# A two-layer encoder trunk: each layer's first projection is v by token tile in place of q and k by halves

## The chip, the cores and the metric

The kernel runs on one core of one Trainium2 chip. A core has a matrix engine (TensorE, PE in the profile), a vector engine (VectorE, DVE), an activation engine (ScalarE, ACT), a general engine (GpSimd, POOL) and a synchronisation engine (SyncE, SP), which here issues nearly all DMAs. Every engine works off its own list of instructions in order; semaphores hold one engine back for another. The metric is the device time of one execution in microseconds (us), the median of several; lower is better.

## The reference, cut to what matters

There is one sequence of 512 tokens with 1024 features, float32, and two layers.

```python
for l in range(DEPTH):                       # 2
    h = rms_norm(x, norm_mix_pre[l], NORM_EPS)
    m = hybrid_mixer(h, w_in[l], w_a[l], w_b[l], w_out[l], lam[l], subln_g[l], cos, sin, lambda_init)
    x = x + rms_norm(m, norm_mix_post[l], NORM_EPS)
    h = rms_norm(x, norm_ffn_pre[l], NORM_EPS)
    f = swiglu(h, w_gate_up[l], w_down[l])
    x = x + rms_norm(f, norm_ffn_post[l], NORM_EPS)
```

`hybrid_mixer` projects h by `w_in` into q, k and v of a differential attention (4 heads with two maps each, `softmax(q0 k0) - lam_full * softmax(q1 k1)`, then a norm with gain `subln_g`), into q, k and v of three groups of windowed attention, and into gates. All q and k are rotated by position (cos, sin). The two attention results go through `w_a` and `w_b`, are gated, added, and projected by `w_out`.

## The kernel before, in words

**Matmuls.** Every product of two fp32 matrices is made of three matmuls on a high and a low part of each operand (high by high, low by high, high by low). A weight block of 256 columns of `w_in` is one DMA of 1 MB into one of two `raw` buffers (`load_raw`, line 88); `split_part` (lines 92 to 112) makes its high part on ACT (`whi`, L106 or L109) and its low part on DVE (`wlo`, L107 or L110). `Stream` (lines 133 to 167) holds the order of the blocks: `cut` splits one and issues the load of the next, `get` hands one out.

**Pre-norm.** A tile is 128 tokens. `prenorm_scale` (lines 242 to 246) squares and sums a tile on ACT (L244), takes the root on DVE and POOL (L73, L75) and scales the tile on DVE (L246). `prenorm_turn` (lines 248 to 256) transposes it on PE in 8 blocks (L252), casts the high part on ACT (L254) and subtracts for the low part on DVE (L255). The result `hTh`, `hTl` has the tokens as columns and is the operand of all projections of a layer. In the head of the program these steps stand in a block in which the ACT and DVE orders are written by hand (lines 395 to 408).

**Projections.** `ws_gen` (lines 199 to 207) multiplies two weight halves with all 512 tokens: 48 matmuls of 512 columns, with a yield after every 12. `ws_halves` (lines 212 to 224) does two such projections with 256 tokens at a time, q and k of the first half, then of the second, so that only the tiles 0 and 1 are needed at first; `between` puts the transposes of tiles 2 and 3 behind the first two pieces. `proj_v` (lines 468 to 480) makes v of a tile with 24 matmuls of 256 columns, and yields after each tile. q and k then go through `rope` (lines 435 to 449): four products on DVE (L446) and two sums on POOL (L447, L448). `split_of` casts the rotated pair on ACT (L485) and subtracts on DVE (L486) for the scores of three of the groups.

**Attention between projections.** `drive` calls `att_step` at every yield of a projection. Each attention is a generator (`da_attn`, `g_attn`) that puts in one step per yield. For a tile of 128 queries, `scores` stands at step 0, `turn` (transposes, L537) at 3, `values` (L546) at 5 and `finish` (transposes of the normed output, L564) at 7; the next tile follows 4 steps later. The scores' 24 matmuls (L511) are followed by the maxima on DVE (L517), exponentials on ACT (L519) and the difference of two maps on DVE (L525, L527). `DELAY` says how many yields lie between an attention's last operand and its first step; its fifth number is added for the first differential attention of a layer.

**Order.** PE's instructions stand as they are written. Those of DVE and ACT are ordered by a scheduler when the program is built, outside of blocks written by hand; `SPLIT_PRI` lets weight splits go ahead.

**Between layers and at the end.** `act_stationary` (lines 293 to 326) is the product with `w_down`, whose last part goes tile by tile; `post` then adds the normed result to x (L267 to L280) and does the next pre-norm. It ends with `ws_halves` of the next two blocks, here q and k of the next layer. The last layer's tiles go out in four DMAs of 32 rows each, by SP (L283).

Of the kernel before, what the change touches and what calls it, by code (L numbers as in the profile page):

```python
# [17 lines left out]
P = 128  # L18
D = 1024
S = 512  # L20
SPLIT_PRI = 400
DELAY = (1, 3, 1, 1, 2)
KT = D // P
NT = S // P
HID = 2816
# [8 lines left out]
def encoder_trunk_kernel(  # L34
# [197 lines left out]
    def class_rows(t, n):  # L232
        return t.rearrange("(t s r) c -> r s t c", s=4, r=4)[n]
# [24 lines left out]
    def postnorm_tile(n, pe, src, g, dst, src_perm, dst_perm, xt=None):  # L258
        if xt is None:
            xt = m4([P, D])  # L260
            rows_in(xt, src, n, src_perm)
        t = m4([P, D])
        ss2 = small(2)
        first, ms = small(1), small(1)

        def msum(ss2):
            nc.vector.scalar_tensor_tensor(out=ms, in0=ss2[:, 1:2], scalar=1.0 / D, in1=first,  # L267
                                           op0=ALU.mult, op1=ALU.add)
            return ms

        for e in range(2):
            sl = slice(e * S, (e + 1) * S)
            nc.scalar.activation(out=junk, in_=pe[e], func=AF.Square, accum_out=ss2[:, e:e + 1])
            if e == 0:
                nc.vector.tensor_scalar(out=first, in0=ss2[:, 0:1], scalar1=1.0 / D, scalar2=NORM_EPS,
                                        op0=ALU.mult, op1=ALU.add)
            nc.vector.tensor_tensor(out=t[:, sl], in0=pe[e], in1=g[:, sl], op=ALU.mult)
        r = small(1)
        nc.gpsimd.tensor_tensor(out=r, in0=msum(ss2), in1=mhalf[:, 0:1], op=ALU.pow)  # L279
        nc.vector.scalar_tensor_tensor(out=xt, in0=t, scalar=r, in1=xt, op0=ALU.mult, op1=ALU.add)  # L280
        if dst_perm:
            for s in range(4):
                nc.sync.dma_start(out=class_rows(dst, n)[s], in_=xt[32 * s:32 * s + 32, :])  # L283
        else:
            nc.sync.dma_start(out=dst[n * P:(n + 1) * P, :], in_=xt)
        return xt, t
# [3 lines left out]
        hTl = pp.tile([P, KT, S], F32R, tag="hTl", name=nm("hTl"))  # L290
        return hTh, hTl

    def act_stationary(nk, lhs, post, turn, next_jobs):
        accs = [[pj(), pj()], [pj(), at(0)], [at(1), at(2)], [at(3), at(4)]]
        nch = nk // 2
        held = []

        def step(n, e, k, hi, lo):
            ah, al = lhs(k, n)
            sl = slice(e * S, (e + 1) * S)  # L300
            o = accs[n][e]
            nc.tensor.matmul(o, ah, hi[:, sl], start=(k == 0), stop=False)  # L302
            nc.tensor.matmul(o, al, hi[:, sl], start=False, stop=False)  # L303
            nc.tensor.matmul(o, ah, lo[:, sl], start=False, stop=(k == nk - 1))  # L304

        for c in range(nch):
            ks = [(2 * c + kk,) + w for kk, w in enumerate(stream.get())]
            if c >= nch - 2:
                held += ks
                continue  # L310
            for kk in ks:
                for n in range(NT):
                    for e in range(2):
                        step(n, e, *kk)
        with (tc.manual_schedule(engines={mybir.EngineType.Activation, mybir.EngineType.DVE})
              if turn is None else nullcontext()):
            for n in range(NT):
                for e in range(2):
                    for kk in held:
                        step(n, e, *kk)  # L320
                    if turn is not None and e == 0 and n >= 2:
                        turn(n - 2)
                post(n, accs[n])
        if turn is None:
            return None
        return ws_halves(next_jobs, 2, {(0, 0): lambda: turn(2), (0, 1): lambda: turn(3)})

    def hT_pairs(hT):
        return [(hT[0][:, k, :], hT[1][:, k, :]) for k in range(KT)]
# [9 lines left out]
    def specs():  # L339
# [10 lines left out]

        for l in range(depth):
            for u in range(2):
                yield from qkv(l, 256 * u, 512 + 256 * u, 1024 + 256 * u)[(1 if l == 0 and u == 0 else 0):]
            for u in range(2):
                for gi in range(3):
                    b = GB + gi * 1536 + 256 * u
                    q, k, v = qkv(l, b, b + 512, b + 1024)
                    yield from (k, v, q) if gi == 0 else (q, k, v)

            def gates(c):  # L360
                return [win(l, ZC + 256 * c, "cols"), win(l, ZC + D + 256 * c, "cols")]
# [24 lines left out]
    nc.sync.dma_start(out=ts0[2][0:1, :], in_=norm_mix_pre[0].unsqueeze(0))  # L386
    rows_in(xt0[0], x0, 0, True)
    nc.sync.dma_start(out=ident, in_=ident_d)
    rows_in(xt0[1], x0, 1, True)
    first_raw = load_raw([wcols(0, w_in, 0)])  # L390
    rows_in(xt0[2], x0, 2, True)
    rows_in(xt0[3], x0, 3, True)
    ones = ts0[1][0:1, 0:P]
    first_w = []
    with tc.manual_schedule(engines={mybir.EngineType.Activation, mybir.EngineType.DVE}):
        nc.vector.memset(ones, 1.0)
        for e in range(2):
            gb = at(e)
            nc.tensor.matmul(gb, ones, ts0[2][0:1, e * S:(e + 1) * S], start=True, stop=True)
            nc.scalar.copy(out=g[:, e * S:(e + 1) * S], in_=gb)  # L400
        prenorm_scale(xt0[0], ts0[0], g)
        prenorm_scale(xt0[1], ts0[1], g)
        prenorm_turn(0, ts0[0], *hT)
        first_w.append(split_part(first_raw, "rope", 0, 0.125))
        prenorm_turn(1, ts0[1], *hT)
        first_w.append(split_part(first_raw, "rope", 1, 0.125))
        prenorm_scale(xt0[2], ts0[2], g)
        prenorm_scale(xt0[3], ts0[3], g)
    head.close()
    hrhs = hT_pairs(hT)  # L410
    first = ws_halves([lambda: (lhs_cols(first_w), hrhs), lambda: (lhs_cols(stream.get()), hrhs)], 2,
                      {(0, 0): lambda: prenorm_turn(2, ts0[2], *hT), (0, 1): lambda: prenorm_turn(3, ts0[3], *hT)})

    for l in range(depth):
        lam_init = 0.8 - 0.6 * math.exp(-0.3 * l)
# [6 lines left out]

        cosb = ip.tile([P, S], F32, tag="cos", name=nm("cos"))
        sinb = ip.tile([P, S], F32, tag="sin", name=nm("sin"))

        def rt():
            return ip.tile([P, 2, S], F32, tag="r", name=nm("r"), bufs=3)
# [29 lines left out]

        oaT = [big() for i in range(2)]

        def proj_qk(which, first):  # L460
            if first is None:
                return (yield from ws_gen(lhs_cols(stream.get()), hrhs))
            if which == 0:
                nc.sync.dma_start(out=cosb, in_=cos_t)
                nc.sync.dma_start(out=sinb, in_=sin_t)
            return first[which]

        def proj_v():
            w2 = stream.get()
# [9 lines left out]
                nc.scalar.copy(out=v[:, 2 * n2:2 * n2 + 2, :], in_=o)  # L479
            return v  # L480

        def split_of(which, natural, first=None):
            pair = rope((yield from proj_qk(which, first)), natural, rt())
            hi, lo = op(), op()
            nc.scalar.copy(out=hi, in_=pair)  # L485
            nc.vector.tensor_tensor(out=lo, in0=pair, in1=hi.bitcast(F32), op=ALU.subtract)  # L486
# [11 lines left out]
            return [(q[0], k[0]), (q[0], k[1]), (q[1], k[0])]  # L498

        def da_proj(first):  # L500
            q = yield from split_of(0, False, first)
            k = yield from split_of(1, False, first)
            return parts_of(q, k), (yield from proj_v())

        def da_attn(u, qk, v):
            st = [dict() for _ in range(NT)]
# [73 lines left out]

        def g_proj(gi):
            if gi == 0:
                k = yield from split_of(1, True)
                v = yield from proj_v()
                vd = dp.tile([S, 256], F32, tag="vd", name=nm("vd"), bufs=2)
                for s in range(4):
# [2 lines left out]
                move(vn, vd.rearrange("(n p) c -> p n c", p=P))  # L589
                vs = m4([P, 3, 256])  # L590
                move(vs, vd[64:448].rearrange("(n p) c -> p n c", p=P))
                q = yield from split_of(0, True)
                return parts_of(q, k), vn, vs
            q = rope((yield from proj_qk(0, None)), False, op(F32))
            k = rope((yield from proj_qk(1, None)), False, op(F32))
            return [(q, k)], (yield from proj_v()), None

        def g_attn(gi, qk, v, vs, res):
# [209 lines left out]
        def post_mix(n, pe):  # L808
# [2 lines left out]

        job = lambda: (lhs_cols(stream.get()), hT_pairs(hT))
        first = act_stationary(KT, lambda k, n: (mg[0][:, k, n * P:(n + 1) * P], mg[1][:, k, n * P:(n + 1) * P]),
                               post_mix, lambda n: prenorm_turn(n, ts[n], *hT), [job, job])
        mid.close()

        fs = ExitStack()
# [40 lines left out]
        if not last:  # L858
            hT = new_hT()
            hT_next = hT  # L860
        job = lambda: (lhs_cols(stream.get()), hT_pairs(hT_next))
        first = act_stationary(NH, act_lhs, post_ffn, None if last else lambda n: prenorm_turn(n, ts[n], *hT_next),
                               [job, job])
        fs.close()


# [46 lines left out]
```

## Time and profile before

| what | value |
|---|---|
| time, median of 3 runs | 1850.47 us (1848.67 to 1851.38) |
| the profiled execution's own time | 1851.76 us |
| its span, first to last instruction | 1850.0 us |
| mean granted TensorE clock in the span | 0.996 |
| mean traffic | 100 GB/s |

The page gives each engine's busy share of the span. The timeline lists an engine's instructions with start and duration, and in brackets the idle time before one and what ended it. A start is counted from the span's start. A matmul's shown duration overlaps the next one's, so starts are compared. The windows view gives busy time and granted clock for a stretch.

### The profile page before, as it was taken

The numbers are of one execution on the slowest core, as the hardware profiler recorded it, in microseconds if no ns is written. First come the engines' busy times: TensorE is split into PE (matmuls) and PEld (weight loads), VectorE is DVE, ScalarE is ACT, GpSimd is POOL, SyncE is SP. The second block draws the span as 40 slices with busy tenths as digits, with TensorE's granted clock in tenths as the row PEclk, the third lists the DMA queues.
The fourth block names the chain that finished last, engine by engine and source line by source line (L and its number), as shares of the span: only waits on it lengthen the run. The fifth ranks groups of instructions, "written<-read, shape, count | busy, mean of one in ns | idle before, by whom it ended". The sixth has DMA issues, their size and how long they took to land. (4 is left out here: it accounts for less than half of the span.)

```text
span 1850.0 us, 25593 instructions
## 1 busy us (share of the span) xinstructions
PE 1822.5 (99%) x10788; PEld 1542.7 (83%) x10788; DVE 916.2 (50%) x1256; ACT 670.1 (36%) x1303; POOL 159.0 (9%) x128
## 2 busy tenths in 40 slices
PE   7999999999999999999999999999999999999998
PEld 6898897888889888888898888888888798888886
DVE  4667667546345333332366676674545543333222
ACT  4454363453234323221344444433533332323221
POOL 1212111101000000000011121111011000000000
PEclk9999999999999999999999999999999999999999
DMA  6322223222344233222442322322224433322231
GB/s 174 96 70 87 70 70 100 70 92 88 126 144 155 92 99 106 91 91 94 157 130 69 101 69 70 101 70 76 85 91 148 159 137 97 108 92 91 93 112 46
DMA packets 145045, 185.74 MB, mean 100 GB/s; under 512 B 7202, under 2 KB 130466, under 8 KB 144931
## 3 DMA queue, kind: packets, MB, share of 16 engines
q1 hardware_dynamic: 144930, 184.11, 31.4%
q8 instruction: 84, 1.38, 0.3%
q14 instruction: 31, 0.25, 0.0%
HBM read 173.54 MB, written 10.55 MB: 100 GB/s over the span
## 5 line engine op out<-in xcount | busy, mean ns | idle before, releaser
L107 DVE TENSOR_TENSOR wlo<-raw,whi 128x1024 fp32r<-128x1024 f32 x252 | 330.3, 1311 | 454.2 <-ACT whi L106 453.8
L121 PE MATMUL pj<-hTh,whi 128*128 128x512 f32 (+1 forms) x1408 | 551.0, 391 | 0.0
L122 PE MATMUL pj<-hTl,whi 128*128 128x512 f32 (+1 forms) x1408 | 543.0, 386 | 0.0
L123 PE MATMUL pj<-hTh,wlo 128*128 128x512 f32 (+1 forms) x1408 | 542.9, 386 | 0.0
L106 ACT CAST whi<-raw 128x1024 fp32r<-128x1024 f32 x252 | 264.6, 1050 | 732.3 <-PE pj L122 476.5
L121 PEld LDWEIGHTS pj<-hTh,whi 128*128 128x128 f32 x1408 | 265.8, 189 | 58.6 <-issue 7.0
L123 PEld LDWEIGHTS pj<-hTh,wlo 128*128 128x128 f32 x1408 | 265.6, 189 | 53.4
L122 PEld LDWEIGHTS pj<-hTl,whi 128*128 128x128 f32 x1408 | 265.8, 189 | 49.7
L121 PE MATMUL pj<-whi,hTh 128*128 128x256 f32 x512 | 147.5, 288 | 0.0
L123 PE MATMUL pj<-whi,hTl 128*128 128x256 f32 x512 | 144.8, 283 | 0.0
L122 PE MATMUL pj<-wlo,hTh 128*128 128x256 f32 x512 | 144.8, 283 | 0.0
L623 ACT ACTIVATE e<-e,gst 128x128 f32<-128x128 f32 (+1 forms) x192 | 81.5, 426 | 81.8 <-DVE gst L620 81.6
L121 PEld LDWEIGHTS pj<-whi,hTh 128*128 128x128 f32 x512 | 98.0, 191 | 3.2 <-issue 2.8
L122 PEld LDWEIGHTS pj<-wlo,hTh 128*128 128x128 f32 x512 | 98.1, 192 | 0.2
L123 PEld LDWEIGHTS pj<-whi,hTl 128*128 128x128 f32 x512 | 98.0, 191 | 0.0
L833 DVE TENSOR_TENSOR s<-s,pj 128x512 f32<-128x512 f32 x42 | 28.9, 689 | 125.2 <-PE pj L123 125.2
L303 PE MATMUL at<-whi,ac 128*128 128x512 f32 x200 | 78.8, 394 | 0.0
L302 PE MATMUL at<-whi,ac 128*128 128x512 f32 x200 | 78.5, 392 | 0.0
L304 PE MATMUL at<-wlo,ac 128*128 128x512 f32 x200 | 77.7, 388 | 0.0
L279 POOL TENSOR_TENSOR sm<-sm,mhalf 128x1 f32<-128x1 f32 x16 | 8.8, 549 | 775.0 <-DVE sm L267 775.0
L519 ACT ACTIVATE e<-at,sm 128x512 f32<-128x512 f32 x64 | 43.8, 688 | 76.4 <-DVE sm L517 76.4
L618 DVE TENSOR_TENSOR e<-at,mk 128x512 f32<-128x512 f32 x64 | 41.3, 684 | 40.3 <-PE at L610 40.3
(188 smaller groups left out, 2531.9 us busy)
## 6 DMA issues: line engine op xcount, KB each, us to landing
raw<-in_w_in_dram SPq DMA_DIRECT2D x64, 1024.0 KB, 5.9
raw<-in_w_gate_up_dram SPq DMA_DIRECT2D x44, 1024.0 KB, 5.1
raw<-in_w_down_dram SPq DMA_DIRECT2D x22, 1024.0 KB, 5.0
raw<-in_w_out_dram SPq DMA_DIRECT2D x8, 1024.0 KB, 4.9
xs<-m SPq DMA_DIRECT2D x12, 512.0 KB, 2.9
m<-xs SPq DMA_DIRECT2D x12, 512.0 KB, 5.2
m<-in_x_dram SPq DMA_DIRECT2D x32, 128.0 KB, 3.4
raw<-in_w_a_dram SPq DMA_DIRECT2D x8, 512.0 KB, 3.5
```

What stands on the lines that cost most here:

```text
L106: nc.scalar.copy(out=shp(hi), in_=src)
L107: nc.vector.tensor_tensor(out=shp(lo), in0=src, in1=shp(hi.bitcast(F32)), op=ALU.subtract)
L121: nc.tensor.matmul(o, ah, bh, start=(i == 0), stop=False)
L122: nc.tensor.matmul(o, ah, bl, start=False, stop=False)
L123: nc.tensor.matmul(o, al, bh, start=False, stop=(i == n - 1))
L302: nc.tensor.matmul(o, ah, hi[:, sl], start=(k == 0), stop=False)
L303: nc.tensor.matmul(o, al, hi[:, sl], start=False, stop=False)
L304: nc.tensor.matmul(o, ah, lo[:, sl], start=False, stop=(k == nk - 1))
L519: nc.scalar.activation(out=e, in_=oc, func=AF.Exp, bias=nmx[:, c:c + 1], accum_out=den[:, c:c + 1])
L618: nc.vector.tensor_tensor(out=e, in0=o[h], in1=mask, op=ALU.add)
L623: nc.scalar.activation(out=e[:, i, :], in_=e[:, i, :], func=AF.Exp, bias=sts[:, n, h:h + 1], accum_out=sts[:, n, 4 + h:5 + h])
L833: nc.vector.tensor_tensor(out=s, in0=s, in1=ou_[i], op=ALU.mult)
```

## The change

The first projection of a layer becomes v, a token tile at a time (`v_first`, `v_mm`). For each tile the 16 matmuls with the high part of the tokens come first (`late` False), then the 8 with the low part (`late` True); `between` puts the transposes of a later tile behind one of these pieces. q and k follow by `ws_gen` in whole width. In the head, SP loads the block of v ahead of x's tile 1 and that of q ahead of tile 3; the gain vector is copied from PSUM by DVE in place of ACT, and the pre-norms of tiles 2 and 3 stand behind the transposes of tiles 1 and 2. The fifth number of `DELAY` goes from 2 to 3. Of the last layer's last tile two of the four DMAs are issued by ACT.

```diff
-DELAY = (1, 3, 1, 1, 2)
+DELAY = (1, 3, 1, 1, 3)
...
             for s in range(4):
-                nc.sync.dma_start(out=class_rows(dst, n)[s], in_=xt[32 * s:32 * s + 32, :])
+                eng = nc.scalar if n == NT - 1 and s % 2 else nc.sync
+                eng.dma_start(out=class_rows(dst, n)[s], in_=xt[32 * s:32 * s + 32, :])
...
+    def v_mm(o, hT, w2, n, late):
+        ns = slice(n * P, (n + 1) * P)
+        for k in range(KT):
+            ah, al = hT[0][:, k, ns], hT[1][:, k, ns]
+            bh, bl = (t[:, (k % 4) * 256:(k % 4 + 1) * 256] for t in w2[k // 4])
+            if late:
+                nc.tensor.matmul(o, al, bh, start=False, stop=(k == KT - 1))
+            else:
+                nc.tensor.matmul(o, ah, bh, start=(k == 0), stop=False)
+                nc.tensor.matmul(o, ah, bl, start=False, stop=False)
+
+    def v_first(w2, hT, between):
+        v = m4([P, NT, 256])
+        for n in range(NT):
+            if n % 2 == 0:
+                o = pj((P, 2, 256))
+            for late in (False, True):
+                v_mm(o[:, n % 2, :], hT, w2, n, late)
+                if (n, late) in between:
+                    between[n, late]()
+            if n % 2 == 1:
+                nc.scalar.copy(out=v[:, n - 1:n + 1, :], in_=o)
+        return v
...
-                yield from qkv(l, 256 * u, 512 + 256 * u, 1024 + 256 * u)[(1 if l == 0 and u == 0 else 0):]
+                q, k, v = qkv(l, 256 * u, 512 + 256 * u, 1024 + 256 * u)
+                yield from (q, k, v) if u else (q, k) if l == 0 else (v, q, k)
...
+    first_raw = load_raw([wcols(0, w_in, 1024)])
     rows_in(xt0[1], x0, 1, True)
-    first_raw = load_raw([wcols(0, w_in, 0)])
     rows_in(xt0[2], x0, 2, True)
+    stream.load()
     rows_in(xt0[3], x0, 3, True)
...
-            nc.scalar.copy(out=g[:, e * S:(e + 1) * S], in_=gb)
+            nc.vector.tensor_copy(out=g[:, e * S:(e + 1) * S], in_=gb)
         prenorm_scale(xt0[0], ts0[0], g)
+        first_w.append(split_part(first_raw, "half", 0))
+        prenorm_turn(0, ts0[0], *hT)
+        first_w.append(split_part(first_raw, "half", 1))
         prenorm_scale(xt0[1], ts0[1], g)
...
+        def then(n, nxt):
+            prenorm_turn(n, ts0[n], *hT)
+            nxt()
+
+        first = v_first(first_w, hT, {
+            (0, False): lambda: then(1, lambda: prenorm_scale(xt0[2], ts0[2], g)),
+            (1, False): lambda: then(2, lambda: prenorm_scale(xt0[3], ts0[3], g)),
+            (1, True): lambda: stream.cut(),
+            (2, False): lambda: prenorm_turn(3, ts0[3], *hT)})
...
+        nc.sync.dma_start(out=cosb, in_=cos_t)
+        nc.sync.dma_start(out=sinb, in_=sin_t)
...
         def da_proj(first):
-            q = yield from split_of(0, False, first)
-            k = yield from split_of(1, False, first)
-            return parts_of(q, k), (yield from proj_v())
+            q = yield from split_of(False)
+            k = yield from split_of(False)
+            return parts_of(q, k), first or (yield from proj_v())
...
         first = act_stationary(NH, act_lhs, post_ffn, None if last else lambda n: prenorm_turn(n, ts[n], *hT_next),
-                               [job, job])
+                               lambda turn: v_first(stream.get(), hT_next, {(0, True): lambda: turn(2),
+                                                                            (2, False): lambda: turn(3)}))
```

What the scheduler makes of it shows in the lists of instructions. First VectorE in the head, before: L732 is the product for `lam`, L742 the scaling of `sg`, L246 the pre-norm's scaling (`m_9` is tile 1, `m_10` tile 2, `m_11` tile 3).

```order
L255 TENSOR_TENSOR hTl_74<-at_155,hTh_73 128x4x128
L110 SCALAR_TENSOR_TENSOR wlo_163<-raw_97,whi_162 128x1024
L73 TENSOR_SCALAR sm_168<-sm_166 128x1
L732 TENSOR_TENSOR e_577<-e_575 128x128
L107 TENSOR_TENSOR wlo_253<-raw_248,whi_252 128x1024
L246 SCALAR_TENSOR_TENSOR m_10_81<-m_6_77,sm_170,g_86 128x1024
L107 TENSOR_TENSOR wlo_257<-raw_248,whi_256 128x1024
L73 TENSOR_SCALAR sm_175<-sm_173 128x1
L734 TENSOR_REDUCE sm_579<-e_577 128x2
L742 TENSOR_SCALAR sg_586<-sg_586 128x128
L246 SCALAR_TENSOR_TENSOR m_11_82<-m_7_78,sm_177,g_86 128x1024
```

And the same place after, where L760 is the product for `lam` and L770 the scaling of `sg`:

```order
L255 TENSOR_TENSOR hTl_74<-pj_136,hTh_73 128x4x128
L107 TENSOR_TENSOR wlo_144<-raw_93,whi_143 128x1024
L73 TENSOR_SCALAR sm_149<-sm_147 128x1
L760 TENSOR_TENSOR e_481<-e_479 128x128
L770 TENSOR_SCALAR sg_490<-sg_490 128x128
L246 SCALAR_TENSOR_TENSOR m_9_80<-m_5_76,sm_151,g_86 128x1024
L762 TENSOR_REDUCE sm_483<-e_481 128x2
L766 TENSOR_TENSOR neglam_487<-sm_485 128x1
L767 TENSOR_SCALAR neglam_487<-neglam_487 128x1
L255 TENSOR_TENSOR hTl_74<-pj_172,hTh_73 128x4x128
```

The two instructions that wait for `lam` and `sg` stood ahead of the scaling of tile 2 and of tile 3; now both stand ahead of that of tile 1.

Second, VectorE around the first scores of the first layer, before. L446 is the rotation of q of the second half (`pj_603` and `pj_604` its two PSUM banks), L107 a weight split, L517 a maximum.

```order
L446 TENSOR_TENSOR r_707<-pj_603,cos_434 128x512
L446 TENSOR_TENSOR r_708<-pj_603,sin_435 128x512
L107 TENSOR_TENSOR wlo_722<-raw_593,whi_721 128x1024
L517 TENSOR_REDUCE sm_669<-at_641 128x1
L517 TENSOR_REDUCE sm_669<-at_642 128x1
L523 RECIPROCAL sm_677<-sm_670 128x2
L517 TENSOR_REDUCE sm_682<-at_643 128x1
L525 SCALAR_TENSOR_TENSOR sm_679<-sm_670,neglam_583,sm_677 128x1
L517 TENSOR_REDUCE sm_682<-at_644 128x1
L527 SCALAR_TENSOR_TENSOR e_672<-e_675,sm_679,e_672 128x512
L446 TENSOR_TENSOR r_707<-pj_604,cos_434 128x512
```

After, L479 is the rotation, L514 the low part of the rotated q, which waits for ACT's cast and that for POOL's sums, and L545 the maximum:

```order
L479 TENSOR_TENSOR r_611<-pj_507,cos_329 128x512
L479 TENSOR_TENSOR r_612<-pj_507,sin_330 128x512
L107 TENSOR_TENSOR wlo_626<-raw_497,whi_625 128x1024
L479 TENSOR_TENSOR r_611<-pj_508,cos_329 128x512
L479 TENSOR_TENSOR r_612<-pj_508,sin_330 128x512
L107 TENSOR_TENSOR wlo_630<-raw_497,whi_629 128x1024
L514 TENSOR_TENSOR op_620<-r_611,op_619 128x1024
L545 TENSOR_REDUCE sm_585<-at_557 128x1
L545 TENSOR_REDUCE sm_585<-at_558 128x1
L551 RECIPROCAL sm_593<-sm_586 128x2
```

The maxima stood ahead of the rotation of the second bank; now they stand behind it and behind L514.

Third, TensorE at the start of the second layer, after: the transposes of tile 3 (L252, `m_1138`) and what stands around them. L302 and L303 are matmuls with the high part of the tokens, L300 those with the low part, `pj_7664` is v of tiles 2 and 3.

```order
L303 MATMUL pj_7664<-wlo_7370,hTh_6821 128x256
L252 MATMUL at_7681<-ident,m_1138_7568 128x128 x4
L252 MATMUL at_7688<-ident,m_1138_7568 128x128 x4
L300 MATMUL pj_7664<-whi_7365,hTl_6822 128x256 x4
L300 MATMUL pj_7664<-whi_7369,hTl_6822 128x256 x4
```

Before, the same transposes stood behind k of the first half of the tokens:

```order
L122 MATMUL at_7688<-hTl_6918,whi_7695 128x256
L123 MATMUL at_7688<-hTh_6917,wlo_7696 128x256
L252 MATMUL at_7819<-ident,m_1138_7664 128x128 x4
L252 MATMUL at_7826<-ident,m_1138_7664 128x128 x4
L128 MATMUL pj_7685<-hTh_6917,whi_7461 128x256
```

They moved forward: 64 matmuls of 256 columns and one tile's transposes stand ahead of them in the layer, where there were 96 and one tile's.

More of the change, by code (lines that the diff above doesn't have):

```diff
@@ L291, in new_hT, with act_stationary @@
         return hTh, hTl
-    def act_stationary(nk, lhs, post, turn, next_jobs):
+    def v_mm(o, hT, w2, n, late):
[20 more added lines that the diff above has]
+        return v
+    def act_stationary(nk, lhs, post, turn, following):
         accs = [[pj(), pj()], [pj(), at(0)], [at(1), at(2)], [at(3), at(4)]]
@@ L325, in act_stationary @@
             return None
-        return ws_halves(next_jobs, 2, {(0, 0): lambda: turn(2), (0, 1): lambda: turn(3)})
+        return following(turn)
     def hT_pairs(hT):
@@ L399, in encoder_trunk_kernel @@
             nc.tensor.matmul(gb, ones, ts0[2][0:1, e * S:(e + 1) * S], start=True, stop=True)
-            nc.scalar.copy(out=g[:, e * S:(e + 1) * S], in_=gb)
+            nc.vector.tensor_copy(out=g[:, e * S:(e + 1) * S], in_=gb)
         prenorm_scale(xt0[0], ts0[0], g)
+        first_w.append(split_part(first_raw, "half", 0))
+        prenorm_turn(0, ts0[0], *hT)
+        first_w.append(split_part(first_raw, "half", 1))
         prenorm_scale(xt0[1], ts0[1], g)
[L403 to L408, printed above, removed]
+        def then(n, nxt):
[6 more added lines that the diff above has]
+            (2, False): lambda: prenorm_turn(3, ts0[3], *hT)})
     head.close()
-    hrhs = hT_pairs(hT)
-    first = ws_halves([lambda: (lhs_cols(first_w), hrhs), lambda: (lhs_cols(stream.get()), hrhs)], 2,
-                      {(0, 0): lambda: prenorm_turn(2, ts0[2], *hT), (0, 1): lambda: prenorm_turn(3, ts0[3], *hT)})
     for l in range(depth):
@@ L458, in encoder_trunk_kernel, with proj_qk @@
         oaT = [big() for i in range(2)]
[L460 to L466, printed above, removed]
+        def proj_qk():
+            return (yield from ws_gen(lhs_cols(stream.get()), hrhs))
         def proj_v():
@@ L480, in proj_v, with split_of @@
             return v
-        def split_of(which, natural, first=None):
-            pair = rope((yield from proj_qk(which, first)), natural, rt())
+        def split_of(natural):
+            pair = rope((yield from proj_qk()), natural, rt())
             hi, lo = op(), op()
@@ L582, in g_proj @@
             if gi == 0:
-                k = yield from split_of(1, True)
+                k = yield from split_of(True)
                 v = yield from proj_v()
@@ L591, in g_proj @@
                 move(vs, vd[64:448].rearrange("(n p) c -> p n c", p=P))
-                q = yield from split_of(0, True)
+                q = yield from split_of(True)
                 return parts_of(q, k), vn, vs
-            q = rope((yield from proj_qk(0, None)), False, op(F32))
-            k = rope((yield from proj_qk(1, None)), False, op(F32))
+            q = rope((yield from proj_qk()), False, op(F32))
+            k = rope((yield from proj_qk()), False, op(F32))
             return [(q, k)], (yield from proj_v()), None
@@ L813, in encoder_trunk_kernel @@
         first = act_stationary(KT, lambda k, n: (mg[0][:, k, n * P:(n + 1) * P], mg[1][:, k, n * P:(n + 1) * P]),
-                               post_mix, lambda n: prenorm_turn(n, ts[n], *hT), [job, job])
+                               post_mix, lambda n: prenorm_turn(n, ts[n], *hT),
+                               lambda turn: ws_halves([job, job], 2, {(0, 0): lambda: turn(2), (0, 1): lambda: turn(3)}))
         mid.close()
@@ L860, in encoder_trunk_kernel @@
             hT_next = hT
-        job = lambda: (lhs_cols(stream.get()), hT_pairs(hT_next))
         first = act_stationary(NH, act_lhs, post_ffn, None if last else lambda n: prenorm_turn(n, ts[n], *hT_next),
-                               [job, job])
+                               lambda turn: v_first(stream.get(), hT_next, {(0, True): lambda: turn(2),
+                                                                            (2, False): lambda: turn(3)}))
         fs.close()
```

## The prediction

> **What bounds the kernel now.** I read the page's busy shares, then the timeline of each engine around every PE gap, then windows with the granted clock.
>
> ```profile
> PE 1822.5 (99%) x10788; PEld 1542.7 (83%) x10788; DVE 916.2 (50%) x1256; ACT 670.1 (36%) x1303; POOL 159.0 (9%) x128
> ```
>
> TensorE is busy 99% of the 1850.0 us span. So the change can act only through what PE itself does (number and width of matmuls), through PE's few idle microseconds, and through its clock. The prices of PE's own work (columns: start, us, engine, line, operation, names, tile, shape, count):
>
> ```profile
> 938.06 1.12 PE L131 MATMUL pj<-hTl,whi 128*128 128x256 f32 x8
> 939.02 1.03 PE L252 MATMUL at<-ident,m 128*128 128x128 f32 x8
> ...
> 970.05 0.40 PE L121 MATMUL pj<-hTh,whi 128*128 128x512 f32 x1
> ...
> 978.33 1.67 PE L511 MATMUL at<-op,op 32*128 32x512 f32 x24
> ```
>
> From start to start, eight 256-wide matmuls take 0.96 us, 0.120 each. From 970.05 to 978.33 run 36 matmuls of 512 columns, 0.23 each; I use 0.228 where nothing else interrupts. Two halves cost 0.240, so the 96 matmuls of q and k in whole width instead of 192 in halves save 1.2 us in a layer. Eight transposes take about 0.9.
>
> The head of the program is where PE waits most:
>
> ```profile
> 23.23 0.29 DVE L732 TENSOR_TENSOR e<-e 128x128 f32<-128x128 f32 x1 [4.57 <-DMA e<-in_lam_dram]
> 24.58 1.28 DVE L246 SCALAR_TENSOR_TENSOR m<-m,sm,g 128x1024 f32<-128x1024 f32 x1
> 27.82 1.28 DVE L246 SCALAR_TENSOR_TENSOR m<-m,sm,g 128x1024 f32<-128x1024 f32 x1 [0.44 <-POOL sm L75]
> 25.91 1.10 PE L252 MATMUL at<-ident,m 128*128 128x128 f32 x8 [2.19 <-DVE m L246]
> ```
>
> VectorE sits 4.57 us on the load of `lam`, and the pre-norm of token tile 2 (L246) stands behind it, so PE idles 2.19 us. Its clock follows (columns: window, length, PE busy and matmuls, granted clock, DMA share, GB/s):
>
> ```profile
> 17.09:20.50 3.41, 3.41 (x18) 0.50 1.01 331
> 20.50:27.33 6.83, 4.64 (x40) 1.00 0.89 293
> 27.33:30.74 3.41, 3.41 (x19) 0.50 0.70 198
> ```
>
> Half clock stands in windows of 3.41 us after idle time. One full of work loses about 1.5 us (18 matmuls where some 28 would fit).
>
> **The change part by part.**
>
> *Head.* Before, PE had tiles 0 and 1 of q to do while `lam` came. Now PE's order is: v of tile 0 (16 matmuls), then the transposes of tile 1. On VectorE, the pre-norm of tile 1 now stands behind both the `lam` product and the scaling of `sg`. When do these land?
>
> ```profile
> 16.80 1.41 SPq L741 DMA_DIRECT2D sg<-in_subln_g_dram  x1
> ...
> sg<-in_subln_g_dram SPq DMA_DIRECT2D x1, 64.0 KB, 6.6
> ```
>
> Issued at 16.80 and 6.6 us under way: 23.4. SP's order of first loads changes, but the bytes ahead of `sg` don't (all of x, two weight blocks, cos, sin, `lam`), and the DMA engines are nearly full up to there (share 0.89 and 1.01 above). I keep 23.4; bounds 19.8 (if it were sooner served, as its light row would allow) to 24.5. Then each tile is a serial loop:
>
> ```profile
> 26.61 1.07 ACT L254 CAST hTh<-at 128x512 fp32r<-128x512 f32 x2 [1.98 <-PE at L252]
> 22.55 1.05 ACT L244 ACTIVATE m<-m 128x1024 f32<-128x1024 f32 x1
> 27.20 0.58 POOL L75 TENSOR_TENSOR sm<-sm,mhalf 128x1 f32<-128x1 f32 x1 [7.91 <-ACT hTh L254]
> 58.49 0.40 PE L121 MATMUL pj<-hTh,whi 128*128 128x512 f32 x1
> ```
>
> `sg` scaled 23.65, L246 of tile 1 to 25.0, its transposes from 25.1. On ACT the square of tile 2 (L244) stands behind the casts of tile 1. So tile to tile: transposes until the second cast can end (0.7, double at half clock, + 1.07), square 1.2, L73 with POOL 0.9, L246 1.28, about 5.1 us, against 24 matmuls and 8 transposes (3.8) on PE. The first turn falls into a half-clock window, 5.8: transposes of tile 2 at 30.9, of tile 3 at 35.9. After these PE has the late part of tile 2 and tile 3, with the casts between, until 40.6, then q and k, 96 x 0.228 = 21.9: the second half's q begins at 62.4 against 58.49, **+3.9**. Bounds: +0.3 (`sg` at 19.8) to +5.0 (at 24.5).
>
> *Attention.* `DELAY` 2 to 3 moves the first scores from three quarters of a projection to its very end. There VectorE's order puts the rotation of the projection's second half, a weight split and the low part of the rotated tile (L486, after: L514) ahead of the maxima of the scores. The trace has this chain, in a place where it harmed little:
>
> ```profile
> 980.02 1.29 DVE L517 TENSOR_REDUCE sm<-at 128x1 f32<-128x512 f32 x2 [1.88 <-PE at L511]
> ...
> 983.63 0.74 DVE L527 SCALAR_TENSOR_TENSOR e<-e,sm,e 128x512 f32<-128x512 f32 x1
> 984.29 0.68 DVE L446 TENSOR_TENSOR r<-pj,cos 128x512 f32<-128x512 f32 x1
> 984.89 1.22 DVE L107 TENSOR_TENSOR wlo<-raw,whi 128x1024 fp32r<-128x1024 f32 x1
> ...
> 987.32 1.74 DVE L527 SCALAR_TENSOR_TENSOR e<-e,sm,e 128x512 f32<-128x512 f32 x1
> 989.62 1.23 DVE L486 TENSOR_TENSOR op<-r,op 128x1024 fp32r<-128x1024 f32 x1 [0.56 <-ACT op L485]
> ...
> 985.12 2.14 POOL L448 TENSOR_TENSOR r<-r,r 128x512 f32<-128x512 f32 x1 [20.79 <-DVE r L446]
> 987.22 1.29 POOL L447 TENSOR_TENSOR r<-r,r 128x512 f32<-128x512 f32 x1
> ...
> 988.54 1.05 ACT L485 CAST op<-r 128x1024 fp32r<-128x1024 f32 x1 [3.12 <-POOL r L447]
> ...
> 988.24 0.60 PE L537 MATMUL at<-ident,e 128*128 128x128 f32 x4
> 989.20 0.63 PE L537 MATMUL at<-ident,e 128*128 128x128 f32 x4 [0.36 <-DVE e L527]
> ```
>
> From the cosine product (984.29) through POOL's two sums and ACT's cast to the end of L486 (990.85) are 6.5 us. Let S be the start of the scores. Before, the first maximum came at S+1.7 (980.02 - 978.33). After, it waits for that chain: S+6.65. From the first maximum to the finished row of head 0 are 4.35 us (984.37 - 980.02), so it is there at S+11.0, and that of head 1, whose steps no rotation parts any more, some 1.3 later. PE asks for them from S+9.9 on (988.24 - 978.33) and stands about 2.0 us in all, in place of some 0.5: **+1.5**. The next tile, at the end of k, also carries the first tile's normed output, for which PE waits in L564:
>
> ```profile
> 82.66 1.29 DVE L517 TENSOR_REDUCE sm<-at 128x1 f32<-128x512 f32 x2 [1.04 <-PE at L511]
> ...
> 92.49 0.61 DVE L557 SCALAR_TENSOR_TENSOR e<-at,sm,sg 128x128 f32<-128x128 f32 x2
> ...
> 80.97 1.67 PE L511 MATMUL at<-op,op 32*128 32x512 f32 x24
> ...
> 93.84 0.38 PE L564 MATMUL at<-ident,e 128*128 128x128 f32 x2
> 189.05 0.44 PE L564 MATMUL at<-ident,e 128*128 128x128 f32 x2 [0.16 <-DVE e L557]
> ```
>
> Before: maximum at S+1.7, output at S+12.1, PE there at S+12.9, no wait. After: the maximum 4.95 later; between, two rotations and a split (2.4) fall away, having gone ahead, and the last L527 runs beside no POOL sum (1.74 becomes 0.74): output at S+13.8; PE, with v's narrower matmuls between, at S+13.1: +0.7. Scores also meet a rotation with cast at the ends of the first window group's k (+0.7) and q (+1.0, an estimate by the same steps with the strided rotation); where they meet v or a rotation without L486 nothing waits. Less the 0.16 above: 3.7 for each of the two layers, **+7.5**. Bounds: 0 (if all meetings are covered) to 10.
>
> *Between the layers.* The same exchange, with other neighbours:
>
> ```profile
> 935.56 0.75 PE L131 MATMUL pj<-hTl,whi 128*128 128x256 f32 x4 [0.99 <-DVE hTl L255]
> 945.64 1.04 PE L252 MATMUL at<-ident,m 128*128 128x128 f32 x8
> ...
> 941.35 1.28 DVE L246 SCALAR_TENSOR_TENSOR m<-m,sm,m 128x1024 f32<-128x1024 f32 x1 [0.66 <-POOL sm L75]
> ```
>
> Gone are about 1.3 us of waiting at 935.56, a few tenths elsewhere, and 1.2 of width. But the transposes of tile 3, before at 945.64 and ready since 942.63, are now due after 64 matmuls and 8 transposes from the start at 931.6, about 940.0: a new wait of 2.7. The net is -0.7. The head's 2.19 us of idle were followed by a half-clock window, so I add one (1.4): **+0.7**. Bounds -1.0 to +1.5. In the Trainium skill, "TensorE: Matmul & The Clock Gate", section "HAM oscillation — how this bites in real kernels", only idle gaps over some 3.4 us bring the half clock back; by that this term is -0.7 and the whole 1.4 lower. The window 27.33 to 30.74, after a gap of 2.19, speaks against it.
>
> *Tail.*
>
> ```profile
> 1845.08 1.71 SPq L283 DMA_DIRECT2D out_dram<-m  x4
> ```
>
> Four issues in a row; two move to ACT's queue, idle then, and the last goes out two issues earlier: **-0.9** (bounds -1.0 to 0, if transfers share engines).
>
> *At nothing:* copying g on VectorE (hidden in the wait for `sg`; 1.3 us without it), the order of the weight splits, ACT's copies of v, attention's end one step later (the gates' projections lie behind it).
>
> Sum: 3.9 + 7.5 + 0.7 - 0.9 = +11.2, so 1863.0 for the profiled run of 1851.76. The median shown is 1.3 lower: **1861.7**.
>
> **Rivals.**
> *Attention is covered* (the maxima overtake on the chip because POOL or ACT end sooner): for it, PE was nearly always fed here; against, the order is fixed and the durations come from the same tiles. 1861.7 - 7.5 = 1854.2.
> *`lam` and `sg` land near 20*, since x now stands partly behind a weight block: 1858.
> *More half clock:* the 2.0 us waits at the end of the second half's q may each bring a window, as 2.19 did: +1.4 a layer, and another in the head: 1865.5.
> *Faster:* nothing that stands ahead on VectorE holds it, in the head or in attention. If `sg` is scaled by 17, the 2.19 of idle and a half-clock window (1.5) go and 1.2 of width is saved, less 2.6 for two turns of the loop (5.1 against 3.8): -2.3; with -0.7 between the layers and -0.9 at the end, 1846.6. In the head it decides at a landing of `sg` 3.9 us before mine, 19.5; in attention at maxima by S+5, when PE would find all rows ready.
>
> **How the numbers follow.** Forecast 0.50 (its own range 1858 to 1865), attention covered 0.14, early landing 0.14, more half clock 0.14, faster 0.08. A measurement tells 0.2% from no change: 1846.8 to 1854.2. Attention covered ends at that line; I count 0.12 of its 0.14 as within, the rest with the other three as slower: faster 0.08, same 0.12, slower 0.80. Range 1853 to 1867: below it lie the faster case and the low half of attention covered; 1867 is the sum of the upper bounds (5.0 + 10 + 1.5).
>
> **What would show it.** In the head: VectorE's L246 of tile 1 just behind the `sg` scaling near 23.6, and PE idle over 6 us before 25. In attention: the first L545 (maximum) near S+6.65, directly behind L514, and PE waiting near 2 us at the next transposes. Between the layers: one PE wait near 2.7 before the last transposes. At the end: two issues on ACT. The sum is wrong if `sg` lands by 20 or L514 does not hold the maxima.

## The result, and the profile after

| | before | after |
|---|---|---|
| time, median of 4 runs each | 1850.93 us | 1873.0 us (1872.95 to 1877.04) |
| ratio, 95% interval | | 1.0124 [1.0112, 1.0137] |
| span of the profiled execution | 1850.0 us | 1871.2 us |

The change makes the kernel slower by 22 us, twice what was forecast and outside the range. The page of the kernel after still names TensorE, with as much busy time as before (1822.5 us then); the 21 us are time in which it stands idle.

```profile
PE 1822.3 (97%) x10596; PEld 1532.7 (82%) x10596; DVE 917.9 (49%) x1258; ACT 674.3 (36%) x1301; POOL 160.7 (9%) x128
```

To see where the time went I compared the start of the same matmul in both traces, at points where the same work lies behind both.

| point | before | after | lag | gained since the point above |
|---|---|---|---|---|
| first layer, second half's q begins | 58.49 | 63.28 | +4.8 | +4.8 (head) |
| first layer, behind the attention's last step | 425.41 | 438.15 | +12.7 | +7.9 (attention) |
| second layer, second half's q begins | 970.05 | 981.97 | +11.9 | -0.8 (between the layers) |
| second layer, behind the attention's last step | 1335.33 | 1356.75 | +21.4 | +9.5 (attention) |
| end of the span | 1850.0 | 1871.2 | +21.2 | -0.2 (last stores) |

In the head, the timeline of VectorE and TensorE after shows the forecast picture: the product for `lam` (L760) and the scaling of `sg` (L770) ahead of tile 1's pre-norm (L246), and TensorE idle behind them.

```profile
24.14 0.29 DVE L760 TENSOR_TENSOR e<-e 128x128 f32<-128x128 f32 x1 [7.46 <-DMA e<-in_lam_dram]
24.34 0.22 DVE L770 TENSOR_SCALAR sg<-sg 128x128 f32<-128x128 f32 x1
24.50 1.28 DVE L246 SCALAR_TENSOR_TENSOR m<-m,sm,g 128x1024 f32<-128x1024 f32 x1
...
25.93 1.08 PE L252 MATMUL pj<-ident,m 128*128 128x128 f32 x4 [7.40 <-DVE m L246]
...
41.50 0.40 PE L121 MATMUL pj<-hTh,whi 128*128 128x512 f32 x1
...
63.28 0.39 PE L121 MATMUL pj<-hTh,whi 128*128 128x512 f32 x1
```

Around the first scores of the second layer (S = 992.94), L514 ends just ahead of the first maximum, which starts at S+6.7. The transposes wait 1.18 and 0.76 us for their rows. The output of a tile (L592) is waited for at the next tile:

```profile
992.94 1.67 PE L539 MATMUL at<-op,op 32*128 32x512 f32 x24
...
998.52 1.23 DVE L514 TENSOR_TENSOR op<-r,op 128x1024 fp32r<-128x1024 f32 x1 [2.27 <-ACT op L513]
999.66 1.28 DVE L545 TENSOR_REDUCE sm<-at 128x1 f32<-128x512 f32 x2
...
1003.26 0.74 DVE L555 SCALAR_TENSOR_TENSOR e<-e,sm,e 128x512 f32<-128x512 f32 x1
...
1004.15 0.63 PE L565 MATMUL at<-ident,e 128*128 128x128 f32 x4 [1.18 <-ACT e L547]
1005.54 1.08 PE L565 MATMUL at<-ident,e 128*128 128x128 f32 x4 [0.76 <-DVE e L555]
...
1024.60 0.44 PE L592 MATMUL at<-ident,e 128*128 128x128 f32 x2 [0.99 <-DVE e L585]
```

What TensorE waited for in the first layer's attention (60 to 240 us), after (columns: engine and line, what it waited for, total us, times, longest):

```profile
PE at L592 <- DVE e L585: 4.0, 4, 1.0
PE at L565 <- ACT e L547: 1.1, 1, 1.1
PE at L565 <- DVE sm L73: 1.0, 2, 0.7
PE at L565 <- DVE e L555: 0.8, 1, 0.8
```

and before, the whole list:

```profile
PE at L537 <- DVE e L527: 0.4, 1, 0.4
PE at L610 <- DVE e L638: 0.2, 1, 0.2
PE at L564 <- DVE e L557: 0.2, 1, 0.2
```

So 0.8 us of waits became 6.9. The lag over the whole attention grew by more. A wait is counted from the shown end of the matmul before it, and the next matmul would have started ahead of that end, so each wait costs some 0.2 us more than it shows (1.2 from start to start for the 1.0 at L592). A wait further on (L686) adds to it, and a half-clock window followed the waits of the first tile. The windows view shows the window with the waits in it and the next one, in both layers:

```profile
83.83:87.24 3.41, 1.51 (x12) 1.00 0.00 0
87.24:90.65 3.41, 3.41 (x11) 0.50 0.02 5
...
1002.01:1005.42 3.41, 1.59 (x9) 1.00 0.00 0
1005.42:1008.84 3.42, 3.30 (x10) 0.50 0.00 0
```

Between the layers the new wait is there with 2.71 us, and at the end two of the last four stores go out by ACT at the same time as SP's:

```profile
955.42 1.09 PE L252 MATMUL at<-ident,m 128*128 128x128 f32 x8 [2.71 <-DVE m L246]
...
1866.47 0.86 ACTq L284 DMA_DIRECT2D out_dram<-m  x2
1866.47 0.78 SPq L284 DMA_DIRECT2D out_dram<-m  x2
```

### The profile page after: what moved, and what is told of

It reads as the page before. It is cut to its first block, busy times and chain, and to the rows that moved or that the text cites. A ratio compares the mean times of both kernels' runs of the same rounds, so it can differ in the third digit from the quotient of the medians.

```text
span 1871.2 us, 25216 instructions
## 1 busy us (share of the span) xinstructions
PE 1822.3 (97%) x10596; PEld 1532.7 (82%) x10596; DVE 917.9 (49%) x1258; ACT 674.3 (36%) x1301; POOL 160.7 (9%) x128
## 5 line engine op out<-in xcount | busy, mean ns | idle before, releaser
L107 DVE TENSOR_TENSOR wlo<-raw,whi 128x1024 fp32r<-128x1024 f32 x252 | 340.1, 1350 | 466.3 <-ACT whi L106 466.0
L121 PE MATMUL pj<-hTh,whi 128*128 128x512 f32 (+1 forms) x1440 | 566.7, 394 | 0.0
L122 PE MATMUL pj<-hTl,whi 128*128 128x512 f32 (+1 forms) x1440 | 558.6, 388 | 0.0
L123 PE MATMUL pj<-hTh,wlo 128*128 128x512 f32 (+1 forms) x1440 | 558.4, 388 | 0.0
L121 PE MATMUL pj<-whi,hTh 128*128 128x256 f32 x448 | 129.7, 289 | 0.0
L122 PE MATMUL pj<-wlo,hTh 128*128 128x256 f32 x448 | 126.7, 283 | 0.0
L123 PE MATMUL pj<-whi,hTl 128*128 128x256 f32 x448 | 126.6, 283 | 0.0
L121 PEld LDWEIGHTS pj<-whi,hTh 128*128 128x128 f32 x448 | 85.7, 191 | 3.9 <-issue 3.5
L122 PEld LDWEIGHTS pj<-wlo,hTh 128*128 128x128 f32 x448 | 85.8, 192 | 0.2
L123 PEld LDWEIGHTS pj<-whi,hTl 128*128 128x128 f32 x448 | 85.8, 192 | 0.0
L110 DVE SCALAR_TENSOR_TENSOR wlo<-raw,whi 128x1024 fp32r<-128x1024 f32 x32 | 44.1, 1382 | 20.7 <-ACT whi L109 20.7
```

The source lines that it names most:

```text
L107: nc.vector.tensor_tensor(out=shp(lo), in0=src, in1=shp(hi.bitcast(F32)), op=ALU.subtract)
L110: nc.vector.scalar_tensor_tensor(out=shp(lo), in0=src, scalar=scale, in1=shp(hi.bitcast(F32)), op0=ALU.mult, op1=ALU.subtract)
L121: nc.tensor.matmul(o, ah, bh, start=(i == 0), stop=False)
L122: nc.tensor.matmul(o, ah, bl, start=False, stop=False)
L123: nc.tensor.matmul(o, al, bh, start=False, stop=(i == n - 1))
```

## The experiments

Names with a_ are made from the kernel after, those with b_ from the kernel before. Ratios are to the kernel before on the same chip.

**The attention delay: undone, and done alone** (a_delay2, b_delay3).

```diff
 a_delay2 (from after)
-DELAY = (1, 3, 1, 1, 3)
+DELAY = (1, 3, 1, 1, 2)
 b_delay3 (from before)
-DELAY = (1, 3, 1, 1, 2)
+DELAY = (1, 3, 1, 1, 3)
```

> The changed kernel with the fifth DELAY back at 2. Theory A (the attention term is the place of the scores at a projection's end): in the changed kernel the two layers lose 7.9 and 9.5 us between the start of the second half's q and the end of attention; all but some 1 us of that goes, and the half-clock window of before (1.4) may return: 1854 to 1858 us. Rival B (the loss comes from v standing first and from the new order of the weight blocks, whatever DELAY is): 1870 to 1875.

> The kernel before with only the fifth DELAY at 3. Theory A: it loses what the changed kernel loses in attention, 15 to 20 us: 1866 to 1870, with PE waiting at the transposes of the scores' rows (about 2 us for the first tile) and at those of the normed output (1.2 to 2.1 for the next). Rival B: 1850 to 1853.

a_delay2: 1856.94 us, ratio 1.0031 [1.0018, 1.0044]. b_delay3: 1869.48 us, ratio 1.0101 [1.0084, 1.0118]. The fifth `DELAY` alone costs 18.5 us where v doesn't come first, and taking it back from the kernel after returns 16. Theory A holds from both sides, and rival B is out. In b_delay3, without any other edit, the waits are those of the kernel after to 0.01 us:

```profile
990.26 1.67 PE L511 MATMUL at<-op,op 32*128 32x512 f32 x24
1001.48 0.63 PE L537 MATMUL at<-ident,e 128*128 128x128 f32 x4 [1.18 <-ACT e L519]
1002.87 1.05 PE L537 MATMUL at<-ident,e 128*128 128x128 f32 x4 [0.77 <-DVE e L527]
...
1022.01 0.44 PE L564 MATMUL at<-ident,e 128*128 128x128 f32 x2 [0.98 <-DVE e L557]
```

**Which instruction holds the scores** (a_lopool).

```diff
             nc.scalar.copy(out=hi, in_=pair)
-            nc.vector.tensor_tensor(out=lo, in0=pair, in1=hi.bitcast(F32), op=ALU.subtract)
+            nc.gpsimd.tensor_tensor(out=lo, in0=pair, in1=hi.bitcast(F32), op=ALU.subtract)
```

> The changed kernel, DELAY 3, with the low part of the rotated q and k (L514) subtracted on GpSimd in place of VectorE; the scores stay where they are. Theory A1 (it is L514's wait, standing ahead of the maxima in VectorE's queue, that makes the scores late): the first maximum comes near S+3.3 in place of S+6.7, PE finds the rows ready at S+9.9, and 10 to 15 us of the 17.4 go: 1858 to 1863. Rival A2 (the scores are late because rotations and weight splits alone fill VectorE there, or because GpSimd's work is the chain): maxima beyond S+5, 1868 or more.

1862.72 us, ratio 1.0063 [1.0048, 1.0078]: 10.3 of the 17.4 us are gone with the scores where they were. The first scores of the first layer there:

```profile
74.50 1.67 PE L539 MATMUL at<-op,op 32*128 32x512 f32 x24
...
77.67 1.27 DVE L545 TENSOR_REDUCE sm<-at 128x1 f32<-128x512 f32 x2
...
80.06 2.39 POOL L514 TENSOR_TENSOR op<-r,op 128x1024 fp32r<-128x1024 f32 x1 [1.16 <-ACT op L513]
...
84.38 0.60 PE L565 MATMUL at<-ident,e 128*128 128x128 f32 x4
85.27 0.63 PE L565 MATMUL at<-ident,e 128*128 128x128 f32 x4 [0.28 <-DVE e L555]
```

The maximum starts at S+3.2, ahead of L514 rather than behind it, and TensorE finds the first row ready at S+9.9. In that layer one wait of 1.0 us at L592 is left of four, and the half-clock window behind the first tile is gone. What stays: the exponentials still stand behind ACT's cast, and the wait at the windowed values (L686) has grown by 1.6 us in each layer; why is open. In the first layer a half-clock window follows that wait (from 280.44 on). From start to start against the kernel after, the matmuls gain some 8.2 us in each layer ahead of L686, of which that wait takes back 1.7 in each and the window 1.5 in the first. So the queue behind L514 makes nearly the whole 17.4. A1 holds, A2 is out.

**The head** (a_lamearly, then a_lam2).

```diff
     nc.sync.dma_start(out=ident, in_=ident_d)
...
+    nc.sync.dma_start(out=lam0, in_=lam[0].rearrange("a b -> (a b)").unsqueeze(0).to_broadcast([P, 4 * DH]))
+    nc.sync.dma_start(out=sg0, in_=subln_g[0].unsqueeze(0).to_broadcast([P, P]))
     first_raw = load_raw([wcols(0, w_in, 1024)])
...
         prenorm_scale(xt0[0], ts0[0], g)
...
+        nc.vector.tensor_tensor(out=lp0, in0=lv0[:, :, 0], in1=lv0[:, :, 1], op=ALU.mult)
...
+        nc.vector.tensor_reduce(out=lsum0, in_=lp0, axis=AX.X, op=ALU.add)
+        nc.vector.tensor_scalar(out=sg0, in0=sg0, scalar1=0.8, scalar2=None, op0=ALU.mult)
         first_w.append(split_part(first_raw, "half", 0))
```

In a_lamearly `sg0` and the result for `lam` are new tiles of 512 and 4 bytes per partition; in a_lam2 they lie in the tile `junk`, which is idle until the first layer's end.

> The changed kernel with the first layer's lam and sg loaded behind the identity, ahead of the first weight block, and used in the head's hand-written order. Theory H (tile 1 waits only for lam and sg): VectorE scales tile 1 near 18.5 in place of 24.5, each further tile 5.1 later unless x is later, and the second half's q starts at 55.5 to 58 in place of 63.3: 1865 to 1868. Rival D (the head is bound by the transfers themselves, tile 3 of x landing at 22.7 in the changed kernel): the last transposes move by under 2 us, 1871 or more.

> As a_lamearly, but the two small operands lie in a buffer that is idle until later, so that no other tile's address moves. In a_lamearly the profile showed the head 6.6 us earlier (v's end at 34.95 in place of 41.50), of which 2.2 were left at the end; the matmuls of the product with w_down ran at 234/234/233 ns in place of 229/232/226. Theory S (those 4 us came from the moved tiles alone): w_down back at 229/232/226, and 1866 to 1867.5 us. Rival (the head's gain is eaten later whatever the addresses): 1870 to 1872.

a_lamearly: 1870.78 us, ratio 1.0112 [1.0095, 1.0129], only 2.2 us better than after. Yet in its trace q begins at 34.95 in place of 41.50: Theory H was right about the head and wrong about the total. From start to start against the kernel after, most of this gain was lost again in the product with `w_down`, 2.0 us in each layer: its matmuls had become slower. Windows over the same 110 us (the number in brackets counts matmuls), first after, then a_lamearly:

```profile
815.00:925.00 110.00, 110.00 (x483) 1.00 0.32 106
```

```profile
815.00:925.00 110.00, 110.00 (x473) 1.00 0.32 110
```

With no other tile moved, a_lam2 gives 1867.77 us, ratio 1.0096 [1.0083, 1.0110]: 5.2 us better than after, and 0.3 above the range of Theory S. Its `w_down` is back at 229, 232 and 226 ns, as it is in a_delay2 and a_lopool, which ran beside a_lamearly. So where the tiles lie is what slowed it, as Theory S has it, and q begins at 35.05:

```profile
35.05 0.40 PE L121 MATMUL pj<-hTh,whi 128*128 128x512 f32 x1
```

It gained 6.5 us in the head of the trace and gave back 1.7 in half-clock windows, which fell elsewhere than in the kernel after: three of them behind the head, where that has two.

**Both causes away** (a_lam2_d2: a_lam2 with the fifth `DELAY` at 2).

> The same with the fifth DELAY at 2: both causes taken away. If they add: 1856.9 - 6.5 = 1850.4, so within 0.2% of the kernel before (range 1848 to 1853). If the two overlap: 1854 or more.

1850.22 us, ratio 1.0000 [0.9991, 1.0009]. The two add, and nothing of the loss is left. What v first has to offer (the width of q and k, the gaps between the layers, the last stores) isn't to be told from zero here.

**Between the layers alone** (b_bound). `v_first`, `v_mm` and the order of the weight blocks of the second layer go with these lines.

```diff
...
-        first = act_stationary(NH, act_lhs, post_ffn, None if last else lambda n: prenorm_turn(n, ts[n], *hT_next),
-                               [job, job])
+        first = act_stationary(NH, act_lhs, post_ffn, None if last else lambda n: prenorm_turn(n, ts[n], *hT_next),
+                               lambda turn: v_first(stream.get(), hT_next, {(0, True): lambda: turn(2),
+                                                                            (2, False): lambda: turn(3)}))
```

> The kernel before with v first at the second layer alone (head, DELAY and last stores as before). From the changed kernel: -0.8 us where no half-clock window follows the new 2.9 us wait; from the run with DELAY 2: +0.4 where one follows. Forecast 1849.8 to 1851.8, not to be told from the kernel before. Rival (the boundary carries a part of the loss): over 1854.

1850.43 us, ratio 1.0003 [0.9994, 1.0012]: no change, as expected. In its trace the second half's q begins 0.25 us later than before. Here the wait of 2.7 us is followed by a half-clock window, which it isn't in the kernel after (below).

**Addresses** (b_pad, b_pad8): an unused tile ahead of all others, set to zero once.

```diff
+    pad = pp.tile([P, 64], F32, tag="pad", name="pad")
+    nc.vector.memset(pad, 0.0)
     junk = pp.tile([P, S], mybir.dt.bfloat16, tag="junk", name="junk")
```

> The kernel before with an unused 256-byte tile (set to zero once) ahead of the other tiles, so that later tiles lie 256 bytes further on. Theory S with any shift: w_down's matmuls go from 229/232/226 to some 233 ns, 2 us a layer, 1854 to 1856. Rival (it was something else in a_lamearly, or 256 bytes are too few or harmless): 1850 to 1852.

> The kernel before with an unused tile of 32 bytes ahead of the others. 256 bytes changed nothing. If a shift that is no multiple of some larger step is what slowed w_down's matmuls in a_lamearly (its two tiles took 512 and 4 bytes): 229/232/226 become some 233 ns and the time 1854 to 1855. If not: 1850 to 1851.

b_pad: 1850.15 us, ratio 0.9998 [0.9989, 1.0007]; b_pad8 (8 columns in place of 64): 1851.56 us, ratio 1.0007 [0.9998, 1.0016]; `w_down` at 229, 232, 226 ns in both. So in the kernel before a shift by 256 or by 32 bytes does no harm, and what about the two tiles of a_lamearly does it stays open; larger shifts were not run.

**A version that beats both** (a_best, a_best2).

```diff
 a_best, from a_lam2_d2
     rows_in(xt0[2], x0, 2, True)
-    stream.load()
     rows_in(xt0[3], x0, 3, True)
+    stream.load()
...
+        prenorm_scale(xt0[2], ts0[2], g)
...
-            (0, False): lambda: then(1, lambda: prenorm_scale(xt0[2], ts0[2], g)),
-            (1, False): lambda: then(2, lambda: prenorm_scale(xt0[3], ts0[3], g)),
+            (0, False): lambda: then(1, lambda: prenorm_scale(xt0[3], ts0[3], g)),
+            (1, False): lambda: prenorm_turn(2, ts0[2], *hT),
 a_best2, from a_best
-            nc.vector.tensor_tensor(out=lo, in0=pair, in1=hi.bitcast(F32), op=ALU.subtract)
+            (nc.vector if natural else nc.gpsimd).tensor_tensor(out=lo, in0=pair, in1=hi.bitcast(F32), op=ALU.subtract)
```

> The changed kernel with lam and sg early, the fifth DELAY at 2, and two more steps in the head: the pre-norm of tile 2 stands ahead of tile 1's transposes (not behind its casts), and x's tile 3 is loaded ahead of the block of q. If the rest of the head is bound by the chain tile after tile, as the trace of the run with both causes removed reads (5 us a tile against 3.8 of matmuls): its head ends some 3 us sooner, 1846.5 to 1849 us, faster than both kernels. If the block of q then comes too late instead: 1850 or more.

> The same, with the low part of the differential attention's q and k on GpSimd (the windowed group's stays on VectorE). If the remaining waits of 0.3 to 0.6 us at the transposes come from VectorE's queue: another 1 to 3 us less. If GpSimd beside VectorE slows its two-operand instructions (1.74 us for the 0.74 of L527 beside a GpSimd sum, in the kernel before): no gain, or up to 2 us more.

a_best: 1847.07 us, ratio 0.9986 [0.9977, 0.9995], faster than both kernels by a little: q begins at 33.24 in its trace, 2.1 us ahead of a_lam2_d2 (35.35), where some 3 had been expected. The two steps weren't tried apart. a_best2: 1848.51 us, ratio 0.9994 [0.9985, 1.0003]: no gain over a_best; in its trace one wait of 1.3 us at L608 (the same transposes of the normed output, L592 after) has appeared in each layer. What brings it was not tested.

## Why the prediction was wrong

*The direction and both causes were right*, and each of its signs was found: L246 of tile 1 directly behind the scaling of `sg`, the first maximum behind L514 (S+6.7 against 6.65), one wait of 2.7 us between the layers, two stores by ACT.

*Head: +3.9 predicted, +4.8 measured.* `lam` landed at 24.1 in place of 23.2 and tile 1's pre-norm began at 24.50 instead of 23.7; the loops took 5.8 and 5.0 as worked out, and so did q and k (21.8). The rows behind the landing of `sg` did not hold: it was issued at 20.48, not 16.80, and was under way for 3.8 us, not 6.6. That it still landed near 24.3, not far from the 23.4 assumed, bears out at most the argument from the bytes ahead of it.

*Attention: +7.5 predicted, +17.4 measured (7.9 and 9.5). This is the step that failed, by its size: 3.7 us for a layer in place of some 9.* The mechanism is shown by b_delay3, a_delay2 and a_lopool, and the first tile's rows were ready nearly as worked out, at S+11.1 and S+12.5 (11.0 and 12.3). Term by term in the second layer, start to start against the same stretch before:

| place | predicted | measured |
|---|---|---|
| first tile's transposes, end of q | 1.5 | 2.1 |
| half-clock window behind it | 0 (a rival: 1.4) | 1.2 |
| its output, end of k | 0.7 | 1.2 |
| first window group, end of k | 0.7 | 1.7 |
| first window group, end of q | 1.0 | 2.1 |
| last tile's output beside the first windowed scores | none | 1.2 |
| windowed values (L686) | none | 0.8 |
| small waits of before, gone | -0.2 | -0.9 |

(In the first layer the half-clock window of before at 317.46 went as well, worth 1.5, hence 7.9 there; that it went was not forecast.) Three things were missed. First, I took the normed output as ready a fixed time behind the maxima. Its own chain starts only behind the whole softmax of the next tile: in VectorE's queue L73 stands behind the last L555, and then POOL and two more steps follow. Before, it stood ahead of the last difference of the two maps (L527); first that, then after:

```profile
1001.37 0.15 DVE L73 TENSOR_SCALAR sm<-sm 128x2 f32<-128x2 f32 x1
1001.48 1.75 DVE L527 SCALAR_TENSOR_TENSOR e<-e,sm,e 128x512 f32<-128x512 f32 x1
```

```profile
1077.07 1.07 DVE L475 TENSOR_TENSOR r<-pj,cos 128x512 f32<-128x512 f32 x1 [2.73 <-PE pj L123]
...
1089.03 0.75 DVE L555 SCALAR_TENSOR_TENSOR e<-e,sm,e 128x512 f32<-128x512 f32 x1
1089.70 0.16 DVE L73 TENSOR_SCALAR sm<-sm 128x2 f32<-128x2 f32 x1
1090.74 0.23 DVE L584 TENSOR_TENSOR sm<-sm,sm 128x1 f32<-128x1 f32 x2 [0.88 <-POOL sm L75]
1090.93 0.61 DVE L585 SCALAR_TENSOR_TENSOR e<-at,sm,sg 128x128 f32<-128x128 f32 x2
...
1091.60 0.44 PE L592 MATMUL at<-ident,e 128*128 128x128 f32 x2 [1.04 <-DVE e L585]
```

Second, at the windowed groups the rotation is strided: L475 takes 1.07 us for the 0.69 of L479, and there I had only estimated. Third, I looked for meetings only where scores meet a rotation, and not at the places further on where the one later step meets the windowed scores and the combination. There it cost 2.0 us a layer:

```profile
1139.51 0.44 PE L592 MATMUL at<-ident,e 128*128 128x128 f32 x2 [1.01 <-DVE e L585]
...
1204.94 1.09 PE L686 MATMUL at<-e,m 128*64 128x128 f32 x16 [1.04 <-ACT m L693]
```

The half-clock window had been set down as a rival with 0.14, and came in both layers of the profiled execution. (By its own terms, 1.4 in each layer and 1.4 in the head, that rival adds up to 1865.9, not 1865.5.)

*Between the layers: +0.7 predicted, -0.8 measured.* The net of matmuls and waits was right (-0.7; the "few tenths elsewhere" have to be 0.9 for it, and the trace of before has 0.4 near 931 and 0.5 near 946.9). The added half-clock window didn't come. The rule of the Trainium skill that was weighed there ("TensorE: Matmul & The Clock Gate", "HAM oscillation — how this bites in real kernels") gave the -0.7. It was not right about the reason, though: in b_bound and a_delay2 the same wait of 2.73 us brought the window.

*Tail: -0.9 predicted, -0.2 measured.* The issues were halved, but the stores of the last two tiles landed 2.0 to 3.0 us after their issue (before: 1.9 to 2.2), so nearly all came back. The Trainium skill says that issuing from several engines saves only the time of issuing ("DMA: Bandwidth & Descriptors", "Issuing engines are not separate DMA queues"); here not even that.

Of the rivals, "early landing" and "faster" are out by the head's trace, "attention is covered" by b_delay3; "more half clock" came true in part, but its sum is 7 us short too.

## What to carry to other kernels

An instruction that waits at the head of an in-order queue costs what stands behind it. So for a change in the order, follow each queue on past the first meeting, to every later step that moved with it, and price the chain that starts only behind the delayed one as well. A step that moves a consumer to the end of its producer's stage gives away the slack that hid the producer's aftermath; here one number in `DELAY` cost some 17 us of the 22. And when two small tiles change more than they should, look at the durations of instructions that weren't touched.

## What the runs showed of the hardware

**The half clock goes by fixed windows.** In every trace the half-clock stretches begin on a grid of 3.413 us: in that of before at 17.09, 27.33 and 317.46, which are 3 and 85 steps apart. Where TensorE had waits between its matmuls of 128 rows, as in all the waits above, half clock follows when it was busy for less than about half of one such window. The same wait of 2.7 us between the layers lay in one window in b_bound and across two after. First b_bound, then after:

```profile
938.50:941.91 3.41, 1.19 (x10) 1.00 1.05 350
941.91:945.33 3.42, 2.91 (x14) 0.50 0.26 101
```

```profile
950.80:954.21 3.41, 1.91 (x16) 1.00 0.99 312
954.21:957.63 3.42, 2.21 (x19) 1.00 0.44 170
957.63:961.04 3.41, 3.41 (x27) 1.00 0.02 5
```

Busy times of 1.19, 1.51 and 1.59 us of 3.41 were followed by half clock, 1.91 and 2.21 were not; the border lies near 1.69, which was followed by half clock in b_delay3 (163.25) and not in a_lamearly (1083.90). The rule doesn't cover all: nine half-clock windows in eight of the traces follow one that was busy for 2.6 to 2.7 us, mostly with the 32-row products of the windowed scores (L610). One of them is that of before at 317.46:

```profile
314.05:317.46 3.41, 2.64 (x45) 1.00 0.10 32
317.46:320.87 3.41, 3.41 (x21) 0.50 0.00 0
```

Another such window, of 2.65 us at 1225.41 in the same trace, was not followed by half clock, and in the heads of b_bound and b_delay3 a second half-clock window came behind a first that was busy for 2.64 and 3.01 us. What decides there stays open. Since the grid starts elsewhere in each execution, a wait of 2 to 3 us costs 1.2 to 1.6 us more in some and nothing in others. The scatter of the runs goes with the clock: of the 27 runs of the kernel before beside a_best, the four with a mean granted clock of 0.999 took 1847.1 to 1848.9 us and the two with 0.996 1852.0. That it is these windows which make the difference is likely, but was not followed run by run.

**Matmuls on moved tiles.** In a_lamearly the `w_down` matmuls, 512 columns wide, took 234, 234 and 233 ns from start to start in place of 229, 232 and 226, at full clock, with nothing changed in them but where tiles lie. That is some 2 us a layer; the cause stays open.

**VectorE beside GpSimd.** The weight split (L107) took 2.00 us while POOL's sums ran and 1.21 when they didn't, in the same attention (at 994.25 and at 1006.51 in the kernel after).
